# Linear attention in paired tiles: both directions, and q and k, by one instruction each

## The chip, the cores and the metric

The kernel runs on one core of a Trainium2 chip. The metric is the device time of one execution in microseconds, as the median of several runs. Five engines of the core work here side by side, each in its own order: TensorE (PE; its weight loads are shown as PEld), VectorE (DVE), ScalarE (ACT), GpSimd (POOL), and SyncE (SP), whose queue issues all of the kernel's loads. An engine goes on to its next instruction only when the one before it could start, so an instruction that waits holds up everything behind it.

## What is computed

The program is a two-layer block over 512 latent tokens behind 256 context tokens (768 in all, 1024 features). Layer 0 mixes tokens by gated linear attention in both directions, layer 1 by neighbourhood attention; a gated MLP with a short convolution follows each. Only layer 0's mixer is changed. Cut to what matters:

```python
def gla_mixer(h_ctx, h_lat, w_in, a_w1, a_w2, a_b, norm_g, w_out, with_ctx_out):
    proj = h @ w_in                                   # h: 768 tokens x 1024
    q, k, v, r = jnp.split(proj, ...)                 # 4 heads: q, k of 128, v, r of 256
    q, k = rope_2d(q[:, L:]) * dk ** -0.5, rope_2d(k[:, L:])
    for d in range(2):                                # both directions
        g = jax.nn.log_sigmoid((h @ a_w1[d]) @ a_w2[d] + a_b[d]) / 16.0
        # S_t = diag(exp(g_t)) S_{t-1} + k_t^T v_t,  o_t = q_t S_t
        o_d, _ = gla_chunked(q, k, v, g, s0)          # d == 1: on the flipped sequence
        o_sum = o_d if o_sum is None else o_sum + o_d
    y = (rms_norm(o, norm_g) * jax.nn.silu(r)).reshape(B, -1, GLA_DV) @ w_out
```

`norm_g` has one weight for each of a head's 256 value features, the same for all heads.

## The kernel before, in words

The kernel is written as tiles (named buffers from pools) and operations on them. The framework gives each engine its order when the program is built: it goes by the order in which the text emits operations, by its own estimates of durations, and by when a buffer is free, and may put an operation that is ready ahead of one emitted earlier. Loads can thus stand in SP's queue long before the text comes to them, as far as staging buffers are free. A tile with `bufs=n` has n buffers; a new one waits for the last reader of the one whose place it takes.

**Projections.** All large products are made of three products of float32r parts (`mm3`, lines 205 to 207: low by high, high by low, high by high). Weights come through `wunit` (190 to 202): a load into a staging tile `st` (line 193, three buffers), a rounded copy on ACT (`wh`, line 200), and the rest on DVE (`wl`, line 201); five pairs of `wh` and `wl` exist.

**Linear attention**, a loop over four heads (683 to 696), has two parts for each head h:

- `part_a(h)`, the levels. A chunk has 128 tokens, and the product of queries and keys inside it is built from seven levels of block size 64, 32, ..., 1. `gates_b` has left the running sums of the log gates of both directions, `b0` and `b1` (128 features x 768 tokens). A level (479 to 511) subtracts from them the value at each block's border, for queries (`eq`) and keys (`ek`), in four operations of 128x384 on DVE (491 to 494); takes the exponential of each on ACT (495, 496); multiplies by q and by k on DVE (497, 498); and multiplies the blocks on PE (`blocks_of`, 463 to 471), whose results go to `att` (504) or `attd` (507). Between levels stand one token tile's value and r projection (`vr_group`, 24 products of 128x512), one quarter of an adaLN vector (`ada_step`, 152 to 174: two loads of `sa`, line 159, two buffers, and sixteen products, line 161), and `silu_r` (557 to 567), which ends with two multiplications on POOL: r by the norm weight `gnB` (566), and by the exponential (567). Head 3 also begins the output projection there (`turn_early`, with transposes at line 591).
- `part_b(h)`, the states: decayed keys (`key_decay`, 513 to 523, for each direction) and queries (`query_decay`, 550 to 555), their transposes (`key_turn`), six chunks' states (`state`, line 542 on PE, 547 on DVE) and outputs (`output`, 578 on PE, then a norm and 584 on DVE). Between these steps stand the next head's q and k projections (`qk_group`, 422 to 434), its rotary (`rope`, 436 to 444: four small DMAs swap halves, lines 440 and 441), its gates (`gates_z`: products at line 399, `e` on ACT at 400, the minimum `mn` on DVE at 401; `gates_b`: exponential 408, logarithm 410, subtraction 411, running sums 415), and its weights. The seam between two heads is what lies around the end of `part_b` and the first level of the next head.

**Buffers that set this order.** One tag, `t3`, of six buffers of 128x768 serves `e`, `mn`, `eq`, `ek`, the decayed keys (two) and queries (two), the turned keys (two) and rope's swap. Five PSUM banks (`ps_aux`) serve the levels, gates, states, outputs, transposes and adaLN sums; three (`ps_mm`) serve the projections. q, k, b0 and b1 have one buffer each.

After the loop the output projection takes `w_go` in two halves of four tiles (675 in head 3's levels, 710 behind the loop), in which a tile of 128 x 1024 holds two groups of 128 features by 512 columns.

Of the kernel before, what the change touches and what calls it, by code (L numbers as in the profile page):

```python
# [9 lines left out]
F32 = mybir.dt.float32  # L10
# [7 lines left out]
N_LAT = 512  # L18
# [14 lines left out]
# row ranges of the packed small vectors  # L33
R_C, R_CC, R_AB, R_N1, R_N2, R_GB, R_CB, R_CW = 0, 8, 16, 112, 128, 144, 152, 196
R_END = 328
# [3 lines left out]
def body(ctx, tc, x, ctx_x, small, ada0, ada, w_gla, a_w1, a_w2, gn, w_go, w_fi, w_fo,  # L39
# [19 lines left out]
    # ---------------------------------------------------------------- constants  # L59
# [37 lines left out]
    # ---------------------------------------------------------------- adaLN vectors  # L97
# [11 lines left out]
    def ada_use(l, o, n, src):  # L109
        """Feature tiles o..o + n of layer l's adaLN vectors, from their products with the conditions."""  # L110
# [14 lines left out]
    def ada_first(q, pool):  # L125
        """256 columns (two feature tiles) of the first two adaLN vectors of layer 0; returns what is left to do."""
# [25 lines left out]
    def ada_step(l, m, i):  # L152
        """Quarter i of the contraction of adaLN vector m of layer l; returns what is left to do with it."""
# [34 lines left out]
    # ---------------------------------------------------------------- helpers  # L188
    def wunit(src, gate=None, eng=None):
        """1024 columns of weights (times a gate for each) as an exact pair of float32r tiles."""  # L190
        n = src.shape[-1]
        st = wst.tile([128, n], F32, name="st", tag="st")
        nc.sync.dma_start(st, src)
# [5 lines left out]
        lo = whl.tile([128, n], FR, name="wl", tag="wl")  # L199
        nc.scalar.activation(hi, st, AF.Copy)  # L200
# [19 lines left out]
    # the features that the projections read, as pairs of float32r: one place for all sub-layers  # L220
# [75 lines left out]
    # ================================================================ layer 0, GLA  # L296
# [44 lines left out]
    with tc.tile_pool(name="gla", bufs=6) as pool:  # L341
        def t3(dt=F32):
            return pool.tile([128, T], dt, name="t3", tag="t3", bufs=6)
# [9 lines left out]
        gnB = pool.tile([128, DV], F32, name="gnB", bufs=1)  # L353
        nc.sync.dma_start(gnB, gn.partition_broadcast(128))
# [9 lines left out]
        # w2 as rows of (high, high, low) parts against the rows (high, low, high) of the low-rank features  # L364
# [26 lines left out]
        def gates_z(h):  # L391
            st[h]["g"] = []
            for d in range(2):
                e = t3()
                mn = t3()
                bias = sT[:, R_GB + 4 * d + h:R_GB + 4 * d + h + 1]
                for a, b in RNG:
                    ps = ps_aux()
                    mm(ps[:, 0:b - a], aw2[:, d, h * 128:(h + 1) * 128], low[d][:, a:b], start=True, stop=True)
                    nc.scalar.activation(e[:, a:b], ps[:, 0:b - a], AF.Abs, bias=bias)  # L400
                    nc.vector.tensor_scalar(mn[:, a:b], ps[:, 0:b - a], bias, 0.0, OP.add, OP.min)
                st[h]["g"].append((e, mn))

        def gates_b(h):
            g = st[h].pop("g")
            st[h]["b"] = []
            for e, mn in g:
                nc.scalar.activation(e, e, AF.Exp, scale=-1.0)
            for d, (e, mn) in enumerate(g):
                nc.scalar.activation(e, e, AF.Ln, bias=1.0)  # L410
                nc.vector.tensor_sub(mn, mn, e)
# [756 lines left out]
```

## Time and profile before

| what | us |
|---|---|
| median of 3 runs | 1770.52 |
| lowest, highest | 1769.62, 1773.61 |
| span of the profiled execution | 1771.4 |
| PE busy in it | 1719.7 |
| DVE busy | 1037.1 |
| ACT busy | 663.7 |
| POOL busy | 319.7 |

The profile is of one execution; its span is 0.9 us above the median of the runs. A matmul's end is modelled in it, so a busy PE is not PE at its peak; a start, and a wait of PE, is what happened. In a group's row the name before the arrow is the tile that is written, those behind it are read; x is the count, then follow the busy time, the mean of one, and the idle time of the engine before them with what ended it. The linear attention's loop lies between about 63 and 420 us of the span.

### The profile page before, as it was taken

To read this page: it belongs to the slowest core of one execution; us is meant where nothing else is said; L and a number is where in the kernel's file an instruction comes from. 1 tells how busy PE (TensorE), PEld (TensorE's weight loads), DVE (VectorE), ACT (ScalarE), POOL (GpSimd) and SP (SyncE) were. 2 spreads that over 40 slices of the span, in tenths; PEclk is the share of its full clock that TensorE was granted. 3 is DMA by queue.
4 is the path that set the end of the run, shared out by engine and by line. 5 is a ranking of instruction groups with operands and counts; after the bars stand their busy time and mean duration, and the time that the engine had idled before them with its cause. 6 is when DMAs were issued, how large, how long until landed. Compare 5 with 4: busy or idle time off the path is not lost.

```text
span 1771.4 us, 27345 instructions
## 1 busy us (share of the span) xinstructions
PE 1719.7 (97%) x11099; PEld 1451.4 (82%) x11099; DVE 1037.1 (59%) x1599; ACT 663.7 (37%) x1225; POOL 319.7 (18%) x474
## 2 busy tenths in 40 slices
PE   6999999999999999999999999999999999999998
PEld 4767676777798999989899978888888788888887
DVE  4697767774646455564655484445445565556555
ACT  4575646552441211212122254443434432233222
POOL 2042323221100000000000023433443202222221
PEclk9999999999999999999999999999999999999999
DMA  8553525331121211212212122133232232333331
GB/s 288 154 192 120 191 84 191 93 111 72 49 95 60 72 60 48 79 59 66 63 57 72 60 66 70 50 100 103 98 107 73 84 106 80 101 107 106 92 100 48
DMA packets 50446, 169.36 MB, mean 96 GB/s; under 512 B 6608, under 2 KB 8528, under 8 KB 50320
## 3 DMA queue, kind: packets, MB, share of 16 engines
q1 hardware_dynamic: 50320, 167.62, 29.3%
q8 instruction: 87, 1.43, 0.3%
q14 instruction: 39, 0.32, 0.1%
HBM read 163.40 MB, written 2.10 MB: 93 GB/s over the span
## 4 chain that ended last, share of the span: by engine, by line
PE 80%; DVE 9%; ACT 3%; issue 2%; DMA 2%; POOL 2%; SPq 0%; DVEq 0%; POOLq 0%; ACTq 0%
PE mm L205 18%; PE mm L206 17%; PE mm L207 17%; PE aux L205 6%; PE aux L207 6%; PE aux L206 6%; PE mm L962 2%; PE aux L945 2%; PE aux L920 2%; DVE t L498 1%; PE aux L161 1%; DVE t L497 1%; PE aux L578 1%; DVE t L492 1%; PE aux L542 1%
## 5 line engine op out<-in xcount | busy, mean ns | idle before, releaser
L205 PE MATMUL mm<-hh,wl 128*128 128x384 f32 (+3 forms) x976 | 344.0, 353 | 3.8 <-ACT hh L217 2.8
L206 PE MATMUL mm<-hl,wh 128*128 128x384 f32 (+3 forms) x976 | 340.6, 349 | 0.4 <-DVE hl L218 0.4
L207 PE MATMUL mm<-hh,wh 128*128 128x384 f32 (+3 forms) x976 | 340.6, 349 | 0.0
L200 ACT ACTIVATE wh<-st 128x1024 fp32r<-128x1024 f32 (+1 forms) x197 | 204.0, 1052 | 317.7 <-issue 179.5
L201 DVE TENSOR_TENSOR wl<-st,wh 128x1024 fp32r<-128x1024 f32 (+1 forms) x196 | 242.7, 1244 | 65.0 <-ACT wh L200 43.0
L205 PEld LDWEIGHTS mm<-hh,wl 128*128 128x128 f32 (+1 forms) x976 | 183.5, 188 | 23.6 <-ACT hh L217 3.5
L206 PEld LDWEIGHTS mm<-hl,wh 128*128 128x128 f32 (+1 forms) x976 | 183.9, 188 | 20.5 <-issue 4.2
L205 PE MATMUL aux<-hh,wl 128*128 128x384 f32 (+2 forms) x576 | 200.5, 348 | 0.0
L207 PE MATMUL aux<-hh,wh 128*128 128x384 f32 (+2 forms) x576 | 200.2, 348 | 0.0
L206 PE MATMUL aux<-hl,wh 128*128 128x384 f32 (+2 forms) x576 | 200.2, 348 | 0.0
L207 PEld LDWEIGHTS mm<-hh,wh 128*128 128x128 f32 (+1 forms) x976 | 184.0, 189 | 15.0
L205 PE MATMUL mm<-wh,ul 128*128 128x512 f32 (+1 forms) x444 | 175.1, 395 | 0.0
L206 PE MATMUL mm<-wl,uh 128*128 128x512 f32 (+1 forms) x444 | 173.7, 391 | 0.0
L207 PE MATMUL mm<-wh,uh 128*128 128x512 f32 (+1 forms) x444 | 172.8, 391 | 0.0
L197 POOL TENSOR_TENSOR st<-st,gB 128x512 f32<-128x512 f32 x60 | 92.6, 1572 | 269.2 <-DMA st<-in 177.5
L788 DVE TENSOR_SCALAR tt<-apad,sT 128x769 f32<-128x769 f32 (+1 forms) x44 | 32.3, 734 | 166.7 <-ACT apad L759 166.7
L245 POOL TENSOR_SCALAR ms<-ss 128x1 f32<-128x1 f32 x26 | 8.8, 340 | 621.0 <-ACT xn L243 620.3
L205 PE MATMUL mm<-wh,hl 128*128 128x512 f32 x288 | 117.7, 409 | 2.3 <-ACT wh L200 1.7
L206 PE MATMUL mm<-wl,hh 128*128 128x512 f32 x288 | 116.0, 403 | 0.0
L205 PEld LDWEIGHTS aux<-hh,wl 128*128 128x128 f32 x576 | 108.3, 188 | 8.9 <-issue 1.8
L207 PE MATMUL mm<-wh,hh 128*128 128x512 f32 x288 | 115.7, 402 | 0.0
L206 PEld LDWEIGHTS aux<-hl,wh 128*128 128x128 f32 x576 | 108.5, 188 | 7.5 <-issue 0.4
(200 smaller groups left out, 2779.4 us busy)
## 6 DMA issues: line engine op xcount, KB each, us to landing
st<-in SPq DMA_DIRECT2D x196, 512.0 KB, 3.6
sa<-in SPq DMA_DIRECT2D x82, 512.0 KB, 4.2
sx<-in SPq DMA_DIRECT2D x14, 512.0 KB, 5.7
xl<-in SPq DMA_DIRECT2D x8, 512.0 KB, 7.7
xc<-in SPq DMA_DIRECT2D x4, 512.0 KB, 4.7
out<-xn SPq DMA_DIRECT2D x8, 256.0 KB, 2.0
raw<-in SPq DMA_DIRECT2D x16, 96.0 KB, 2.4
t<-q SPq DMA_DIRECT2D x16, 64.0 KB, 3.6
```

Of the source, the lines that this page charges most:

```text
L161: mm(ps[32 * j:32 * j + 32, 0:256], cs[:, k, :], st[:, 256 * j:256 * j + 256], start=k == 0, stop=k == KD - 1, skip_group_check=True)
L197: nc.gpsimd.tensor_mul(st[:, s_], st[:, s_], gate[half])
L200: nc.scalar.activation(hi, st, AF.Copy)
L201: (eng or nc.vector).tensor_sub(lo, st, hi.bitcast(F32))
L205: mm(out, a[1], b[0], start=first, stop=False)
L206: mm(out, a[0], b[1], start=False, stop=False)
L207: mm(out, a[0], b[0], start=False, stop=last)
L492: nc.vector.tensor_sub(v(eq)[:, :, 0, :], v(bB)[:, :, 0, :], cB)
L788: nc.vector.tensor_scalar(tt, ap_[:, 1:1 + m], cw[1], cb, OP.mult, OP.add)
L920: mm(pss[hh][:, off:off + 256], qe[a_][p_, 128 * t:128 * t + 128], ke[b_][p_, ks], start=i == 0, stop=i == 2)
L945: nc.tensor.transpose(pT[:, i * 128:(i + 1) * 128], S2[:, o:o + 128], ident)
L962: mm(po[64 * hh:64 * hh + 64, 128 * t:128 * t + 128], V[:, vs[i], 64 * hh:64 * hh + 64], PTs[hh][:, i * 128:(i + 1) * 128], start=i == 0, ...
```

## The change

Three things, all in layer 0's mixer:

- *Pairs.* Tiles of 128 x 768 become tiles of 128 x 2 x 768 (`t6`, three buffers in place of `t3`'s six): e and mn for both directions; the gates' running sums in one tile `bb`, backward first; q and k in one tile `qk`; a level's `eq` and `ek`; decayed keys, turned keys and decayed queries for both directions. One instruction then does for both what two did: the exponential, logarithm and subtraction of the gates, the exponential and the multiplication of a level, of the keys' decay and of the queries' decay. A level's four subtractions become two of 128x768, through an access pattern written by hand that steps between the two halves of `bb`; for keys the order of the subtraction is turned round, so that one scale serves both exponentials. Rope's swap gets a tile of its own with one buffer.
- *Norm weights.* `gnB`, its load and the POOL multiplication by it go. The norm weight comes as two columns with the packed small vectors and multiplies the rows of `w_go` as these are converted: in two halves on ACT (with a scale) and on DVE (scalar_tensor_tensor).
- *Loads.* The loads of the next head's q and k weights are emitted behind the first products of `part_a`, ahead of the levels; their conversion stays behind the levels.

Comments are removed too. The core of the diff:

```diff
+    def wload(src):
+        st = wst.tile([128, src.shape[-1]], F32, name="st", tag="st")
+        nc.sync.dma_start(st, src)
+        return st
...
+        if scales:
+            for half in range(2):
+                s_ = slice(half * 512, half * 512 + 512)
+                nc.scalar.activation(hi[:, s_], st[:, s_], AF.Copy, scale=scales[half])
+                nc.vector.scalar_tensor_tensor(lo[:, s_], st[:, s_], scales[half], hi[:, s_].bitcast(F32), OP.mult,
+                                               OP.subtract)
+            return hi, lo
...
-        def t3(dt=F32):
-            return pool.tile([128, T], dt, name="t3", tag="t3", bufs=6)
+        def t6():
+            return pool.tile([128, 2, T], F32, name="t6", tag="t6", bufs=3)
...
         def gates_z(h):
+            e, mn = t6(), t6()
             for d in range(2):
...
-                    nc.scalar.activation(e[:, a:b], ps[:, 0:b - a], AF.Abs, bias=bias)
-                    nc.vector.tensor_scalar(mn[:, a:b], ps[:, 0:b - a], bias, 0.0, OP.add, OP.min)
+                    nc.scalar.activation(e[:, d, a:b], ps[:, 0:b - a], AF.Abs, bias=bias)
+                    nc.vector.tensor_scalar(mn[:, d, a:b], ps[:, 0:b - a], bias, 0.0, OP.add, OP.min)
...
+            e, mn = st[h].pop("g")
+            nc.scalar.activation(e, e, AF.Exp, scale=-1.0)
+            nc.scalar.activation(e, e, AF.Ln, bias=1.0)
+            nc.vector.tensor_sub(mn, mn, e)
+            bb = pool.tile([128, 2, T], F32, name="bb", tag="bb", bufs=1)
...
+                    nc.vector.tensor_tensor_scan(bb[:, 1 - d, a:b][:, ::step], reset, mn[:, d, a:b][:, ::step], 0.0,
                                                  OP.mult, OP.add)
...
+        def qk_load(h):
+            st[h]["raw"] = [wload(w_gla[h, i]) for i in range(2)]
...
-            sw = t3()
+            sw = pool.tile([128, N_LAT], F32, name="sw", tag="sw", bufs=1)
...
         def level(h, li):
...
-            nc.vector.tensor_sub(v(eq)[:, :, 1, :], v(bF)[:, :, 1, :], cF)
-            nc.vector.tensor_sub(v(eq)[:, :, 0, :], v(bB)[:, :, 0, :], cB)
-            nc.vector.tensor_sub(v(ek)[:, :, 0, :], v(bF)[:, :, 0, :], cF)
-            nc.vector.tensor_sub(v(ek)[:, :, 1, :], v(bB)[:, :, 1, :], cB)
-            nc.scalar.activation(eq, eq, AF.Exp, scale=1.0 / GATE)
-            nc.scalar.activation(ek, ek, AF.Exp, scale=-1.0 / GATE)
-            nc.vector.tensor_mul(eq, eq, st[h]["q"])
-            nc.vector.tensor_mul(ek, ek, st[h]["k"])
+            def at(first, second, inner=1):
+                return bass.AP(bb.tensor, base + first, [lead, [2 * s, n], [second - first, 2], [inner, s]])
+            e = t6()
+            eq, ek = (e[:, i, :].rearrange("p (n two s) -> p n two s", two=2, s=s) for i in range(2))
+            nc.vector.tensor_sub(eq, at(0, T + s), at(s, T + s - 1, 0))
+            nc.vector.tensor_sub(ek, at(T + s - 1, s, 0), at(T, s))
+            nc.scalar.activation(e, e, AF.Exp, scale=1.0 / GATE)
+            nc.vector.tensor_mul(e, e, st[h]["qk"])
...
         def key_decay(h):
+            kd = t6()
+            for d in range(2):
+                nc.vector.tensor_sub(ch(kd[:, d, :]), ch(bb[:, 1 - d, :]),
+                                     last[:, d, :, :].to_broadcast([128, NCH, CH]))
             nc.scalar.activation(kd, kd, AF.Exp, scale=-1.0 / GATE)
+            nc.vector.tensor_mul(kd, kd, st[h]["qk"][:, 1:2, :].to_broadcast([128, 2, T]))
...
         def silu_r(h, c):
...
-            nc.gpsimd.tensor_mul(yh, yh, gnB)
             nc.gpsimd.tensor_mul(yh, yh, e)
...
             diag(h)
+            if h < HEADS - 1:
+                qk_load(h + 1)
             for i in range(7):
                 level(h, i)
...
-                wo[0] = [wunit(w_go[0, q]) for q in range(4)]
+                wo[0] = [wunit(w_go[0, q], scales=gn_cols) for q in range(4)]
```

More of the change, by code (lines that the diff above doesn't have):

```diff
@@ L34, with body @@
 R_C, R_CC, R_AB, R_N1, R_N2, R_GB, R_CB, R_CW = 0, 8, 16, 112, 128, 144, 152, 196
-R_END = 328
+R_GN = 328
+R_END = 330
 @with_exitstack
-def body(ctx, tc, x, ctx_x, small, ada0, ada, w_gla, a_w1, a_w2, gn, w_go, w_fi, w_fo,
+def body(ctx, tc, x, ctx_x, small, ada0, ada, w_gla, a_w1, a_w2, w_go, w_fi, w_fo,
          w_nqk, w_no, rpb, fg, ident_d, rope_d, lvl_d, nmask_d, *outs):
@@ L186, in gate_rows, with wunit @@
         return out
-    def wunit(src, gate=None, eng=None):
+    def wload(src):
+        st = wst.tile([128, src.shape[-1]], F32, name="st", tag="st")
+        nc.sync.dma_start(st, src)
+        return st
+    def wunit(src, gate=None, eng=None, scales=None):
         n = src.shape[-1]
-        st = wst.tile([128, n], F32, name="st", tag="st")
-        nc.sync.dma_start(st, src)
+        st = wload(src) if src.space == bass.MemoryType.DRAM else src
         if gate:
@@ L352, in body @@
         nc.vector.tensor_copy(lvl, lst)
-        gnB = pool.tile([128, DV], F32, name="gnB", bufs=1)
-        nc.sync.dma_start(gnB, gn.partition_broadcast(128))
+        gn_cols = [sT[:, R_GN + i:R_GN + i + 1] for i in range(2)]
         two_i = pool.tile([128, 32], F32, name="two_i", bufs=1)
@@ L525, in key_turn, with key_decay @@
-        def key_turn(h, d):
-            kd = st[h].pop(("kd", d))
-            kt = t3()
-            for c0, c1 in ((0, 4), (4, 6)):
+        def key_decay(h):
+            bb = st[h]["b"]
+            last = bass.AP(bb.tensor, bb.offset + T + CH - 1, [bb.ap[0], [1 - CH - T, 2], [CH, NCH], [0, 1]])
+            ed = sml.tile([128, 2, NCH], F32, name="ed", tag="ed", bufs=2)
+            nc.scalar.activation(ed, last.rearrange("p d c o -> p d (c o)"), AF.Exp, scale=1.0 / GATE)
+            kd = t6()
+            for d in range(2):
+                nc.vector.tensor_sub(ch(kd[:, d, :]), ch(bb[:, 1 - d, :]),
+                                     last[:, d, :, :].to_broadcast([128, NCH, CH]))
+            nc.scalar.activation(kd, kd, AF.Exp, scale=-1.0 / GATE)
+            nc.vector.tensor_mul(kd, kd, st[h]["qk"][:, 1:2, :].to_broadcast([128, 2, T]))
+            st[h]["kd"] = kd
+            st[h]["ed"] = ed
@@ L529, in key_turn @@
+        def key_turn(h):
+            kd = st[h].pop("kd").rearrange("p d t -> p (d t)")
+            kt = t6()
+            st[h]["kt"] = kt
+            kt = kt.rearrange("p d t -> p (d t)")
+            for c0 in range(0, 2 * NCH, 4):
                 ps = ps_aux()
-                for c in range(c0, c1):
+                for c in range(c0, c0 + 4):
                     nc.tensor.transpose(ps[:, (c - c0) * CH:(c - c0 + 1) * CH], kd[:, c * CH:(c + 1) * CH], ident)
-                nc.scalar.activation(kt[:, c0 * CH:c1 * CH], ps[:, 0:(c1 - c0) * CH], AF.Copy)
@@ L533, in key_turn @@
-            st[h]["kt", d] = kt
-            st[h]["S", d] = {}
+                nc.scalar.activation(kt[:, c0 * CH:c0 * CH + 512], ps, AF.Copy)
+            for d in range(2):
+                st[h]["S", d] = {}
         ORDER = ((0, 1, 2, 3, 4, 5), (1, 0, 5, 4, 3, 2))
@@ L541, in state @@
             ps = ps_aux()
-            mm(ps[:, 0:DV], st[h]["kt", d][:, c * CH:(c + 1) * CH], st[h]["v", c], start=True, stop=True)
+            mm(ps[:, 0:DV], st[h]["kt"][:, d, c * CH:(c + 1) * CH], st[h]["v", c], start=True, stop=True)
             s_new = pool.tile([128, DV], F32, name=f"S{d}", tag=f"S{d}", bufs=5 if d else 3)
@@ L546, in state @@
             else:
-                nc.vector.scalar_tensor_tensor(s_new, S[c], st[h]["ed", d][:, c, :], ps[:, 0:DV], OP.mult, OP.add)
+                nc.vector.scalar_tensor_tensor(s_new, S[c], st[h]["ed"][:, d, c:c + 1], ps[:, 0:DV], OP.mult, OP.add)
             S[order[i + 1]] = s_new
         def query_decay(h):
-            for d in range(2):
-                e = t3()
-                nc.scalar.activation(e, st[h]["b"][d], AF.Exp, scale=1.0 / GATE)
-                nc.vector.tensor_mul(e, e, st[h]["q"])
-                st[h]["qd", d] = e
+            e = t6()
+            nc.scalar.activation(e, st[h]["b"], AF.Exp, scale=1.0 / GATE)
+            nc.vector.tensor_mul(e, e, st[h]["qk"][:, 0:1, :].to_broadcast([128, 2, T]))
+            st[h]["qd"] = e
         def silu_r(h, c):
@@ L709, in finish_gla @@
             add_gated(pool, ps, (g_ctx if t < 2 else g_lat)[0], X[t][:, 0:512])
-        wo[1] = [wunit(w_go[1, q]) for q in range(4)]
+        wo[1] = [wunit(w_go[1, q], scales=gn_cols) for q in range(4)]
         for t in range(6):
```

71 lines of the change are left out of this document (21 added, 50 removed).

## The prediction

> **What bounds the kernel now.** I read the page first, then busy time by stretch, the waits of TensorE (PE), the chain of work that ended last, and the order of time on VectorE (DVE) and on the DMA queue of SyncE (SP). The page's first lines:
>
> ```profile
> span 1771.4 us, 27345 instructions
> PE 1719.7 (97%) x11099; PEld 1451.4 (82%) x11099; DVE 1037.1 (59%) x1599; ACT 663.7 (37%) x1225; POOL 319.7 (18%) x474
> L200 ACT ACTIVATE wh<-st 128x1024 fp32r<-128x1024 f32 (+1 forms) x197 | 204.0, 1052 | 317.7 <-issue 179.5
> ```
>
> PE is busy 97% of the span, so an edit off PE can only win back PE's waits. 1771.4 - 1719.7 = 51.7 us is the most there is, and the change touches only the linear attention. By stretch (start:end, length, then busy PE, PEld, DVE, ACT, POOL, and PE's granted clock), head 0's levels, head 1's levels, head 1's states, head 3's levels:
>
> ```profile
> 90.00:124.00 34.00, 30.97 (x487) 19.22 (x486) 33.36 (x51) 23.73 (x47) 11.66 (x11) 1.00 0.57 184
> 165.00:207.00 42.00, 39.86 (x535) 28.97 (x535) 41.69 (x63) 29.75 (x59) 12.21 (x10) 1.00 0.44 138
> 207.00:252.00 45.00, 41.28 (x262) 34.27 (x261) 21.69 (x35) 17.76 (x40) 9.77 (x16) 0.92 0.43 141
> 338.00:380.00 42.00, 39.59 (x555) 28.78 (x551) 41.32 (x64) 29.48 (x60) 13.60 (x13) 1.00 0.32 101
> ```
>
> In the levels DVE is busy 41.69 of 42.00 us and PE 39.86: both are nearly full, DVE a little fuller. In the states DVE has half its time free and PE waits 45.00 - 41.28 = 3.7 us. PE's waits over the whole linear attention (total, times, longest), the chain at the seam of head 1, and SP's issues there:
>
> ```profile
> PE aux L161 <- DMA sa<-in: 8.4, 7, 3.7
> PE aux L469 <- DVE t L498: 6.3, 7, 1.4
> PE aux L591 <- DVE attd L507: 2.3, 1, 2.3
> ```
>
> ```profile
> 205.10 1.14 DVE wl L201
> 206.69 5.06 DMA sa<-in
> 211.79 1.08 PE aux L161 x8
> ```
>
> ```profile
> 151.66 0.38 SPq L193 DMA_DIRECT2D st<-in  x1
> 204.26 2.33 SPq L193 DMA_DIRECT2D st<-in  x2
> 206.69 1.31 SPq L159 DMA_DIRECT2D sa<-in  x2
> ```
>
> One late engine makes two waits. PE waits 6.3 us for level products (L469) because DVE is full. It waits 8.4 us for adaLN weights (sa) because SP, in order, holds their issue behind weight loads (st), and those wait for a staging buffer that DVE's conversion (L201) frees. So the bound is DVE in the levels, and what shortens DVE there counts until PE itself is full.
>
> **Fewer, larger instructions.** DVE back to back without disturbance, and the two exponentials of a level on ScalarE (ACT):
>
> ```profile
> 256.83 0.56 DVE L491 TENSOR_TENSOR t<-b 128x384 f32<-128x384 f32 x1
> 257.29 0.96 DVE L497 TENSOR_TENSOR t<-t,q 128x768 f32<-128x768 f32 x1
> 258.16 0.95 DVE L498 TENSOR_TENSOR t<-t,k 128x768 f32<-128x768 f32 x1
> ```
>
> ```profile
> 256.01 0.85 ACT L495 ACTIVATE t<-t 128x768 f32<-128x768 f32 x1 [1.14 <-DVE t L492]
> ```
>
> From start to start a 384-wide operation takes 257.29 - 256.83 = 0.46 (0.47 with the unrounded rest) and a 768-wide one 258.16 - 257.29 = 0.87 us. Each 384 more cost 0.40, and 0.07 is fixed, so a 1536-wide one takes 1.67. A level has four subtractions and two multiplications, 4 x 0.47 + 2 x 0.87 = 3.62; afterwards two and one, 2 x 0.87 + 1.67 = 3.41. Seven levels save 7 x 0.21 = 1.5. The decays' four multiplications become two: 3.48 - 3.34 = 0.1. Together 1.6 us of DVE per head.
>
> [...] The starts decide: the durations overlap, and 0.07 is what an instruction costs.
>
> **The norm weight's multiplication leaves POOL.** While POOL multiplies, DVE's operations take longer. DVE and POOL in head 1's levels (us busy, mean ns):
>
> ```profile
> L497 DVE TENSOR_TENSOR t<-t,q 128x768 f32<-128x768 f32 x7 | 7.2, 1027 | 0.0
> L498 DVE TENSOR_TENSOR t<-t,k 128x768 f32<-128x768 f32 x7 | 7.1, 1010 | 0.0
> ...
> L494 DVE TENSOR_TENSOR t<-b 128x384 f32<-128x384 f32 x7 | 4.9, 706 | 0.0
> L492 DVE TENSOR_TENSOR t<-b 128x384 f32<-128x384 f32 x7 | 4.9, 706 | 0.0
> L493 DVE TENSOR_TENSOR t<-b 128x384 f32<-128x384 f32 x7 | 4.4, 628 | 0.0
> L491 DVE TENSOR_TENSOR t<-b 128x384 f32<-128x384 f32 x7 | 4.4, 627 | 0.0
> L521 DVE TENSOR_TENSOR t<-t,k 128x768 f32<-128x768 f32 x2 | 2.4, 1224 | 0.0
> ```
>
> ```profile
> L566 POOL TENSOR_TENSOR xl<-xl,gnB 128x256 f32<-128x256 f32 x3 | 3.4, 1123 | 15.6 <-DVE er L564 15.6
> L567 POOL TENSOR_TENSOR xl<-xl,er 128x256 f32<-128x256 f32 x3 | 3.2, 1066 | 0.2
> ```
>
> Against the undisturbed 0.555 and 0.955 us these are too long by 7 x (0.072 + 0.055 + 0.151 + 0.151 + 0.073 + 0.072) + 2 x 0.269 = 4.6 us per head. A head's r takes twelve POOL multiplications, six of them by gnB (L566). Without these six DVE gets back between 0 and 4.6; I take half, 2.3, since L566 and L567 are alike in size and duration. DVE's relief is 1.6 + 2.3 = 3.9 us per head, 15.6 for four.
>
> **The gates between heads get later.** The seam after head 1, on DVE and on PE:
>
> ```profile
> 244.57 1.14 DVE L401 TENSOR_SCALAR t<-aux,sT 128x384 f32<-128x384 f32 x2
> ...
> 246.80 1.15 DVE L401 TENSOR_SCALAR t<-aux,sT 128x384 f32<-128x384 f32 x2
> 247.86 0.48 DVE L584 SCALAR_TENSOR_TENSOR xl<-aux,rs,xl 128x256 f32<-128x256 f32 x1
> 248.25 0.86 DVE L547 SCALAR_TENSOR_TENSOR S<-S,ed,aux 128x256 f32<-128x256 f32 x2
> 249.03 1.80 DVE L415 TENSOR_TENSOR_SCAN b<-reset,t 128x384 f32<-128x384 bf16 x2
> 250.75 0.94 DVE L411 TENSOR_TENSOR t<-t,t 128x768 f32<-128x768 f32 x1
> ```
>
> ```profile
> 245.43 0.59 PE L542 MATMUL aux<-V,t 128*128 128x256 f32 x2
> ...
> 246.09 0.59 PE L542 MATMUL aux<-V,t 128*128 128x256 f32 x2
> ...
> 246.75 0.39 PE L207 MATMUL mm<-wh,hh 128*128 128x512 f32 x1
> 246.98 0.40 PE L205 MATMUL mm<-wh,hl 128*128 128x512 f32 x1
> ```
>
> Six single buffers become three double ones. At the seam they hold the decayed queries, the turned keys and e; mn needs the turned keys' buffer, free after the last state (L542, 246.09 + 0.59 = 246.7). Today one direction's minimum has run by then (244.57), and the other waits (246.80). Afterwards both wait. After the release DVE has two minima more (247.86 - 246.80 = 1.06) and a doubled L411 (0.80), but L584 and one L547 (0.39 + 0.39) fall before it: 1.1 later. Also, the four gate products hold four of five aux banks until their minima; today the two at 244.57 free the banks in which the states at 245.43 and 246.09 run. Afterwards the states share the bank of the output before them, free after its L584, now at about 246.8 + 0.5 = 247.3. Two states in turn, each 0.59 on PE with a 0.5 evacuation between, end at 249.0, not 246.7: 2.3 later. The bank's share lies between 0 (another order) and 2.3; the nearest rows are these, so I take 2.3. That is 3.4 us per seam, 10.2 for three. Queued behind it on DVE are the scans and all of the next levels; PE has value products meanwhile.
>
> **The rest.** In head 0 the doubled L411 stands ahead of the scans: +0.8. The scaled output weights cost ACT a second start: from 0.85 at 768 columns and 1.052 at 1024 (0.79 ns a column) a start is 0.24, four times 1.0 us for the first half's weights, where PE already waits 2.3 (L591); between 0 and 1.0, I take 0.5. The second half's conversions stand beside a full PE: 0, otherwise 1.0. Rope's single swap buffer makes k's swap follow q's: hidden in head 0 by four subtractions of level 0 (1.9, the cost without that cover). The early q and k loads, moved ahead of the levels' 14 adaLN loads on SP, I cost at 0: the staging buffers are already filled that early, the last at 151.66, with the next issue at 204.26 only when conversions free one. Fewer key-turn copies, one decay factor instruction and the gnB load gone: off the path, 0.
>
> **Sum**: -15.6 + 10.2 + 0.8 + 0.5 = -4.1 us on the chain through DVE. PE can follow: head 0 (-3.9 + 0.8) has 34.00 - 30.97 = 3.0 us of waits, the others need 3.9 - 3.4 = 0.5 each. The profiled span is 0.9 us above the median of the runs, 1770.5 (1769.6 to 1773.6); the difference is applied to that: 1766.4.
>
> **Rivals.** (1) *The adaLN wait falls too*: if the build's order lets DVE's conversion gain on PE by the 3.9 us of a head, the 8.4 us of sa waits go, and so does the half clock that follows:
>
> ```profile
> 211.30:218.00 6.70, 6.21 (x30) 4.06 (x31) 0.10 (x1) 0.56 (x2) 2.11 (x4) 0.50 0.75 243
> ```
>
> 6.7 us at 0.50 lose 3.4. Then -4.1 - 8.4 - 3.4 = -15.9: 1754.6. For it: the chain. Against it: after head 0 a head's net gain is 0.5 us, not 3.9. [...]
>
> (2) *Nothing is won*: larger pieces expose latency. A level's first product waits for a 1.45 us exponential (0.85 + 768 x 0.79 ns) and a 1.67 us multiplication where pieces overlapped; 0.6 + 0.8 later at each of four heads is 5.6, which eats the 4.1 and 1.5 more: 1772. For it: PE's waits for L498. Against it: DVE has other levels to do, three in flight as now.
>
> (3) *Slower, by the banks*: a state that wants the one free bank is placed on PE behind a group of 24 value products (one each 246.98 - 246.75 = 0.23 us, so 5.5). The seam is then 8.9 later; in two seams of three that is 11.0 more, and -4.1 becomes +6.9: 1777. It turns the sign from 4.1 / 3 = 1.4 us per seam beyond my 3.4. Against it: PE's rows show states put between single value products.
>
> **How the numbers follow.** A measurement here can tell about 0.2%, 3.5 us. The forecast has 0.45 (1762 to 1770.5, of which 0.28 beyond 3.5 us faster), rival 1 0.17, rival 2 0.18, rival 3 0.20. Faster 0.28 + 0.17 = 0.45; within 0.2% 0.17 + 0.16 = 0.33; slower 0.20 + 0.02 = 0.22. The range of 8 in 10 runs from 1752 (rival 1 and 2 us) to 1777 (the price of rival 3).
>
> **What would show it.** Right: L566 gone and the level subtractions' means near 0.96 us; DVE's busy time in the levels down by some 4 us; minima (L401) in one run of four after the last state. Wrong: levels as full as before, PE waiting for states' banks, or sa waits gone altogether.

## The result, and the profile after

The changed kernel takes 1774.68 us (median of 18 runs, 1771.42 to 1777.69) against 1771.22 us (18 runs beside them, 1765.49 to 1774.06): a ratio of 1.0019, 95% interval [1.0011, 1.0027]. It is slower by 0.19%, 3.4 us. The forecast was 4.1 us faster. The medians of the kernel before, on the chips used here, lie between 1770.8 and 1771.8, so kernels are compared below by their ratios to the runs of the kernel before on the same chip; 0.1% is 1.8 us.

The profiled execution after, its span and the share of each engine:

```profile
span 1773.1 us, 27174 instructions
...
PE 1718.0 (97%) x11099; PEld 1447.0 (82%) x11099; DVE 1022.4 (58%) x1511; ACT 658.1 (37%) x1181; POOL 324.8 (18%) x450
```

DVE has lost 88 instructions and 14.7 us of busy time over the whole program. The forecast's 15.6 is another sum (start to start, in the four heads), but of the same size, and the kernel is still no faster. POOL has 24 instructions fewer and is busy 5.1 us longer. The stretches that answer to those shown of before (start:end, length, then busy PE, PEld, DVE, ACT, POOL, and the granted clock), from the first to the last block product of a head: head 0's levels, head 1's levels, its states up to the next head's first block product, head 3's levels:

```profile
76.40:124.50 48.10, 42.95 (x572) 30.83 (x571) 42.03 (x47) 32.59 (x58) 11.85 (x5) 0.96 0.45 139
165.80:209.20 43.40, 40.27 (x577) 28.32 (x576) 40.52 (x45) 28.79 (x53) 16.77 (x9) 1.00 0.42 131
209.20:254.70 45.50, 42.37 (x229) 35.18 (x225) 19.65 (x32) 17.54 (x36) 7.69 (x13) 0.96 0.43 143
342.60:387.30 44.70, 41.10 (x551) 28.57 (x550) 39.71 (x48) 28.18 (x55) 16.08 (x9) 0.96 0.35 107
```

Head 1's levels before, cut in the same way:

```profile
162.80:205.10 42.30, 40.16 (x580) 28.97 (x579) 41.55 (x65) 29.51 (x61) 13.73 (x13) 1.00 0.40 126
```

They have grown from 42.3 us to 43.4 although DVE in them does less, and POOL, with half of its multiplications gone, is busy 16.77 us in them. PE's waits, then POOL's last multiplication of silu_r (mean ns after the comma, first two token tiles and the others), then ACT's waits for it:

```profile
PE aux L162 <- DMA sa<-in: 14.1, 14, 2.5
PE aux L481 <- DVE t L507: 6.0, 4, 1.9
PE aux L557 <- DVE xl L597: 1.8, 3, 0.6
```

```profile
L580 POOL TENSOR_TENSOR xc<-xc,er 128x256 f32<-128x256 f32 x8 | 40.4, 5067 | 61.6 <-ACT er L579 61.6
L580 POOL TENSOR_TENSOR xl<-xl,er 128x256 f32<-128x256 f32 x16 | 19.0, 1188 | 54.4 <-ACT er L579 54.1
```

```profile
ACT er L575 <- POOL xc L580: 15.7, 5, 6.7
```

The last two in the kernel before:

```profile
L567 POOL TENSOR_TENSOR xl<-xl,er 128x256 f32<-128x256 f32 x16 | 17.2, 1074 | 1.3
L567 POOL TENSOR_TENSOR xc<-xc,er 128x256 f32<-128x256 f32 x8 | 9.7, 1207 | 5.7 <-ACT er L565 5.3
```

```profile
ACT er L561 <- POOL xc L567: 2.1, 2, 1.7
```

Three things stand out. The wait for adaLN weights (sa) did not fall; it rose from 8.4 to 14.1 us. The wait for level products is as it was, 6.3 and now 6.0. And POOL's multiplication lasts 5.07 us on average on the first two tiles (1.21 before), so that ACT, in order, stands still for its result for 15.7 us, where it was 2.1 before.

The seam after head 1, on DVE and on PE, shows what the prediction had foreseen:

```profile
249.36 0.48 DVE L597 SCALAR_TENSOR_TENSOR xl<-aux,rs,xl 128x256 f32<-128x256 f32 x1 [3.26 <-POOL rs L226]
250.64 0.48 DVE L562 SCALAR_TENSOR_TENSOR S<-S,ed,aux 128x256 f32<-128x256 f32 x1 [0.79 <-PE aux L557]
251.91 2.19 DVE L412 TENSOR_SCALAR t<-aux,sT 128x384 f32<-128x384 f32 x4 [0.79 <-PE aux L557]
...
261.41 0.95 DVE L504 TENSOR_TENSOR t<-bb 128x768 f32<-128x768 f32 x1
```

```profile
249.90 0.70 PE L557 MATMUL aux<-V,t 128*128 128x256 f32 x2 [0.61 <-DVE xl L597]
...
251.18 0.70 PE L557 MATMUL aux<-V,t 128*128 128x256 f32 x2
...
254.73 0.26 PE L481 MATMUL aux<-qk 128*32 128x32 f32 x6
```

All four minima (L412) run in one go, right behind the last state (251.18 + 0.70), and DVE idles ahead of them. States wait for the bank that an output holds (0.61). From the first turned key to the end of the last state it is now 251.9 - 219.0 = 32.9 us (29.9 before). The next head's first level subtraction (L504) starts 261.41 - 254.73 = 6.7 us behind its first block product. In head 1 that distance was 3.7 us before (L491 at 166.45, first block product at 162.8).

### The profile page after: what moved, and what is told of

The parts are those of the page before. It is cut to its first block, busy times and chain, and to the rows that moved or that the text cites. A ratio compares the mean times of both kernels' runs of the same rounds, so it can differ in the third digit from the quotient of the medians.

```text
span 1773.1 us, 27174 instructions
## 1 busy us (share of the span) xinstructions
PE 1718.0 (97%) x11099; PEld 1447.0 (82%) x11099; DVE 1022.4 (58%) x1511; ACT 658.1 (37%) x1181; POOL 324.8 (18%) x450
## 4 chain that ended last, share of the span: by engine, by line
PE 85%; DMA 4%; DVE 3%; POOL 2%; issue 2%; ACT 2%; DVEq 0%; SPq 0%; POOLq 0%; ACTq 0%
PE mm L218 18%; PE mm L220 18%; PE mm L219 18%; PE aux L218 6%; PE aux L219 6%; PE aux L220 6%; DMA sa<-in 4%; PE aux L162 2%; PE mm L975 2%; PE aux L933 2%; PE aux L958 1%; PE aux L591 1%; PE aux L557 1%; DVE bb L425 1%; PE aux L284 1%
## 5 line engine op out<-in xcount | busy, mean ns | idle before, releaser
L213 ACT ACTIVATE wh<-st 128x1024 fp32r<-128x1024 f32 (+1 forms) x189 | 196.0, 1052 | 302.6 <-issue 179.5
L214 DVE TENSOR_TENSOR wl<-st,wh 128x1024 fp32r<-128x1024 f32 (+1 forms) x188 | 234.6, 1253 | 62.2 <-ACT wh L213 40.7
L801 DVE TENSOR_SCALAR tt<-apad,sT 128x769 f32<-128x769 f32 (+1 forms) x44 | 31.9, 725 | 165.8 <-ACT apad L772 165.8
```

Source lines behind the costliest of these rows:

```text
L214: (eng or nc.vector).tensor_sub(lo, st, hi.bitcast(F32))
L801: nc.vector.tensor_scalar(tt, ap_[:, 1:1 + m], cw[1], cb, OP.mult, OP.add)
```

## The experiments

Each was timed in five rounds beside the kernel before. Theory A is POOL's starved multiplication with ACT behind it, theory B the seam between heads, theory C the two buffers of the adaLN weights.

**POOL out of the levels (e1, e2).** The first moves one multiplication, the second the whole of silu_r.

```diff
-            nc.gpsimd.tensor_mul(yh, yh, e)
+            nc.vector.tensor_mul(yh, yh, e)
```

> The changed kernel with silu_r's one multiplication (yh by e) on DVE instead of POOL: no POOL work in the levels. Theory A (POOL's multiplication is starved by DVE's back-to-back merged instructions, and ACT, in order, waits for the er buffer that it holds): ACT's wait for POOL (15.7 us over the kernel) is gone, at the price of 6 x 0.48 = 2.9 us of DVE per head less the 2.1 of contention that was left, so some 0.8 us more DVE per head; the kernel is 2 to 6 us faster than the changed one, about 1769 to 1773. Theory B (the seam between heads carries the loss: the gates' minima wait for the turned keys' buffer, states share a bank): the seams stay and DVE only gets more to do, 1775 to 1780. Theory C (the two adaLN buffers bind by themselves): PE's waits for sa stay near 14 us and the time near 1775.

Measured: 1768.8 us, ratio 0.9984 [0.9972, 0.9996], 6 us faster than the changed kernel. ACT's waits for POOL are gone; PE's sa waits stay at 13.7.

```diff
 # part_a
-                if i > 0:
-                    silu_r(h, i - 1)
 # part_b: silu_r(h, 0), (h, 1) after other(0); (h, 3) after other(1); (h, 4) after other(2); (h, 2), (h, 5) after other(3)
```

> The changed kernel with all of silu_r moved from the levels to the states, ahead of the outputs that use it, where DVE has half its time free. Theory A: the levels lose the POOL contention (2.1 us per head), ACT's waits for POOL, and 6 x 0.4 = 2.4 us of DVE per head, so they become PE-bound at some 41 us instead of 43.4 to 48; time 1758 to 1768. Theory B: the seam, already the cost, gets 6 x 4 ACT activations of about 0.45 us (10.8 us) more per head in ACT's order ahead of key turns and state copies: 1776 to 1785. Theory C: sa waits stay at 14 us, the levels shorten little, 1772 to 1776.

Measured: 1766.9 us, 0.9963 [0.9948, 0.9978], 10 us faster by the ratio, within A's range. So taking POOL's multiplication out of the levels is worth 6 us in the changed kernel, and taking all of silu_r out, with ACT's and DVE's part of it, 10 us. It is not the whole loss, as the next runs show.

**The parts by themselves (e3, e4).** e3 takes the kernel before and drops gnB's multiplication, with the output weights scaled as in the change. e4 is the change without that part; a multiplication of the same size by the cosine table stands in for the one by gnB, and the norm weights are left out of its result.

```diff
 # e3, in the kernel before
-            nc.gpsimd.tensor_mul(yh, yh, gnB)
...
-                wo[0] = [wunit(w_go[0, q]) for q in range(4)]
+                wo[0] = [wunit(w_go[0, q], scales=gn_cols) for q in range(4)]
 # e4, in the changed kernel
+            nc.gpsimd.tensor_mul(yh, yh, cosT[:, 0:DV])
             nc.gpsimd.tensor_mul(yh, yh, e)
```

> The kernel before with the norm weight's part alone: gnB's multiplication gone from silu_r, output weights scaled, tiles and loads as before. Theory A: DVE's instructions stay small and leave gaps, so POOL's remaining multiplications still take about 1.1 us, ACT does not wait, and DVE gets back about half of its 4.6 us of contention per head: 1762 to 1768. Theory B: it has nothing to do with the seam, so the gain of 1762 to 1768 would come too, and the loss must then show in the next kernel. Rival D (scaling the output weights costs what it saves): 1770 to 1773.

> The changed kernel with a second multiplication of the same size back on POOL in silu_r (by the first 256 columns of the cosine table in place of the norm weights) and the output weights unscaled, so paired tiles and early loads without the norm weight's part; the norm weights are not applied. Theory A: two starved multiplications per chunk, ACT waits longer for POOL than the 15.7 us of the changed kernel; 1778 to 1786. Theory B: the seams are the loss and unchanged, DVE's contention as before the change: 1775 to 1779. Theory C: like the changed kernel, 1773 to 1776.

Measured: e3 1759.7 us, 0.9925 [0.9907, 0.9942]; e4 1781.2 us, 1.0045 [1.0032, 1.0059]. The norm weights' part alone gains 0.75%, 13 us, and the tiles in pairs cost 8 us without it and 0.94%, 17 us, on top of it. So the change is a gain and a larger loss, and the loss lies in the pairs. Head 0's and head 1's levels in e3 (columns as above), and POOL's multiplication in it:

```profile
76.00:121.00 45.00, 42.00 (x581) 28.27 (x580) 41.96 (x68) 32.38 (x67) 6.79 (x6) 1.00 0.49 156
159.40:201.30 41.90, 40.05 (x580) 28.95 (x579) 40.42 (x66) 30.56 (x63) 7.75 (x8) 1.00 0.43 137
```

```profile
L573 POOL TENSOR_TENSOR xc<-xc,er 128x256 f32<-128x256 f32 x8 | 9.4, 1178 | 76.9 <-ACT er L572 76.9
```

Beside DVE's small instructions POOL needs 1.18 us, not 5.07.

**The levels' instructions unmerged (e5).** Pair tiles, loads and scaled weights stay.

```diff
-            nc.vector.tensor_sub(eq, at(0, T + s), at(s, T + s - 1, 0))
-            nc.vector.tensor_sub(ek, at(T + s - 1, s, 0), at(T, s))
-            nc.scalar.activation(e, e, AF.Exp, scale=1.0 / GATE)
-            nc.vector.tensor_mul(e, e, st[h]["qk"])
+            def one(off, inner=1):
+                return bass.AP(bb.tensor, base + off, [lead, [2 * s, n], [inner, s]])
+            nc.vector.tensor_sub(eq[:, :, 1, :], one(T + s), one(T + s - 1, 0))
+            nc.vector.tensor_sub(eq[:, :, 0, :], one(0), one(s, 0))
+            nc.vector.tensor_sub(ek[:, :, 0, :], one(T + s - 1, 0), one(T))
+            nc.vector.tensor_sub(ek[:, :, 1, :], one(s, 0), one(s))
+            for i in range(2):
+                nc.scalar.activation(e[:, i, :], e[:, i, :], AF.Exp, scale=1.0 / GATE)
+            for i in range(2):
+                nc.vector.tensor_mul(e[:, i, :], e[:, i, :], st[h]["qk"][:, i, :])
```

> The changed kernel with the paired tiles, early loads and scaled output weights kept, but a level's instructions as before: four subtractions of 384, two exponentials and two multiplications of 768, each on its half of the paired tile. Theory A (the long two-input instructions without gaps starve POOL): POOL's multiplication, 5.07 us mean on the first two chunks now, returns to 1.2 to 1.5, ACT's 15.7 us of waits for it fall to 2, DVE has 1.5 us per head more to do; 3 to 9 us faster than the changed kernel, 1766 to 1772. Theory B (the seam: shared buffers and banks) and theory C (two adaLN buffers, early loads): POOL may be served sooner, but the time stays, 1774 to 1778.

Measured: 1773.7 us, 1.0012 [0.9998, 1.0027], no different from the changed kernel. POOL and ACT in it:

```profile
L587 POOL TENSOR_TENSOR xl<-xl,er 128x256 f32<-128x256 f32 x16 | 31.3, 1957 | 57.9 <-ACT er L586 57.7
L587 POOL TENSOR_TENSOR xc<-xc,er 128x256 f32<-128x256 f32 x8 | 11.8, 1470 | 82.8 <-ACT er L586 82.8
```

```profile
ACT er L582 <- POOL xc L587: 3.7, 2, 3.3
```

On the first tiles POOL's delay goes with the long instructions: with short ones its multiplication is back to 1.47 us there (5.07), and ACT's wait falls from 15.7 to 3.7, while on the other tiles it takes 1.96 (1.19). The time does not follow, against what A expected: whatever merging saved on DVE and whatever it cost through POOL come out even here.

**The gates in one buffer (e6, and e11 and e15 as controls).** -ln(1 + exp(-z)) needs no second tile; the signs of the later exponentials turn. e6 has no guard against overflow, which the minimum is in the original; in e11 (the kernel before) and e15 (e3) z is kept above -80 by the same instruction.

```diff
-            e, mn = t6(), t6()
+            e = t6()
...
-                    nc.scalar.activation(e[:, d, a:b], ps[:, 0:b - a], AF.Abs, bias=bias)
-                    nc.vector.tensor_scalar(mn[:, d, a:b], ps[:, 0:b - a], bias, 0.0, OP.add, OP.min)
+                    nc.vector.tensor_scalar(e[:, d, a:b], ps[:, 0:b - a], bias, None, OP.add)
...
-            nc.vector.tensor_sub(mn, mn, e)
```

> The changed kernel with the gates' logarithm of the sigmoid as -ln(1 + exp(-z)), without the guard of the minimum against overflow: one paired tile instead of two, no minimum's buffer that waits for the turned keys, 1.7 us less DVE per seam. Theory A: the seam gives back 1 to 3 us of its 3.65, POOL is starved as in the changed kernel: 1768 to 1773, less than half of the way to the 1759.7 of the norm weights alone. Theory B: the seam falls back to that of the kernel before and the time with it: 1762 to 1767. Theory C: 1773 to 1775.

> The kernel before with the gates as -ln(1 + exp(-z)), z kept above -80 by the same instruction, so one tile per direction and no minimum and no subtraction: the control to the same edit of the changed kernel, which gained 20 us. Theory B1 (the buffer's wait in the paired tiles): no such wait here, only some 3 us of DVE less per head beside free DVE time: 1766 to 1770. Theory B2 (fewer instructions at the seam): 1752 to 1760.

> The kernel before with the norm weights' part and the gates in one tile per direction (z kept above -80), so the run with the gates in one buffer (1754.6 us) without paired tiles. If pairing is worth its 6 us once the seam's wait is gone: 1758 to 1762. If pairing gains nothing: 1752 to 1756. If it still costs: 1746 to 1751.

Measured: e6 1754.6 us, 0.9901 [0.9884, 0.9917], faster than any theory had it; e11 1761.4 us, 0.9939 [0.9920, 0.9957], between B1 and B2; e15 1755.0 us, 0.9901 [0.9878, 0.9924]. The edit gains 21 us in the changed kernel and 11 in the one before, but in e3, which differs from the changed kernel by the pairs (and the early loads) alone, it gains only 0.24%, 4 us (each of these to within 3 to 5 us). So shorter gates are worth some 4 us there, and the other 17 hang on the second paired tile that the gates no longer need: as much as the pairs cost on top of e3. With the gates in one buffer, pairs (e6) and no pairs (e15) take the same time. The 6 us by which pairs ought to have won are not there either.

**The wait by itself (e9).** The cleanest run: no instruction fewer, only another tile for the minima, one that is free since the query decay.

```diff
-            e, mn = t6(), t6()
+            e = t6()
+            mn = pool.tile([128, 2, T], F32, name="bb", tag="bb", bufs=1)
...
-            bb = pool.tile([128, 2, T], F32, name="bb", tag="bb", bufs=1)
+            bb = mn
```

> The changed kernel with the gates' minima written into the tile in which the scans end (free since the query decay, scanned in place) instead of a third paired buffer: same instructions, no wait for the turned keys' buffer. Theory B1 (the minima's wait for that buffer, with the banks that the gate products hold meanwhile, is the loss of the seams): key turn to last state falls from 31 to 33 us back to 29 or less and the time to 1756 to 1766. Theory B2 (the gain of the run with one buffer came from its 1.7 us less of DVE and four activations fewer per seam): 1771 to 1775. Theory A (POOL): 1771 to 1775 too.

Measured: 1760.3 us, 0.9935 [0.9918, 0.9953], 0.84% or 15 us faster than the changed kernel, of the 17 that the pairs cost. The seam after head 1 on DVE, then head 1's levels and its states:

```profile
236.32 2.19 DVE L413 TENSOR_SCALAR bb<-aux,sT 128x384 f32<-128x384 f32 x4
...
250.62 0.95 DVE L505 TENSOR_TENSOR t<-bb 128x768 f32<-128x768 f32 x1
```

```profile
164.20:205.60 41.40, 39.67 (x580) 29.09 (x579) 36.48 (x42) 29.76 (x52) 5.79 (x5) 1.00 0.43 141
205.60:249.50 43.90, 41.36 (x224) 34.53 (x223) 22.95 (x35) 16.66 (x36) 9.74 (x17) 0.96 0.44 145
```

The minima run at 236.32, 5.3 us ahead of the last state's end (241.6). The first level subtraction follows the first block product by 250.62 - 249.50 = 1.1 us, not 6.7. That is less than the 3.7 of the kernel before: e9 takes away more than the pairs had added, since in the kernel before one direction's minimum waited too. In the levels DVE is busy 36.48 of 41.40 us: it has room again. In head 1 POOL is quick too:

```profile
173.43 0.94 POOL L581 TENSOR_TENSOR xc<-xc,er 128x256 f32<-128x256 f32 x1 [11.52 <-ACT er L580]
182.39 0.94 POOL L581 TENSOR_TENSOR xc<-xc,er 128x256 f32<-128x256 f32 x1 [8.03 <-ACT er L580]
```

In the levels of heads 1 and 3 POOL is busy 5.79 and 6.09 us, where it was 16.77 and 16.08 in the changed kernel. So there the starving goes with the wait. That POOL starves because DVE is late is not shown, though: in e6, whose gates are early, POOL's mean on the first tiles is still 3.6 us, and only ACT's waits for it are gone (1.3 us):

```profile
L578 POOL TENSOR_TENSOR xc<-xc,er 128x256 f32<-128x256 f32 x8 | 28.8, 3606 | 62.1 <-ACT er L577 62.1
```

The sa waits in e9 fall to 7.6.

**On top of it (e13, e14).** e13 is e9 with e1's edit, e14 is e9 with e5's.

> The run with the minima in the scans' tile (1760.3 us), and silu_r's multiplication on DVE besides. If POOL's hold on ACT in head 0 (one wait of 6.6 us there) still costs: 2 to 5 us faster than that run, 1755 to 1758. If DVE's 2.9 us more per head weigh as much: 1759 to 1762.

> The run with the minima in the scans' tile, and the levels' instructions unmerged as in the kernel before. If merging shortens the levels as the prediction reckoned (1.5 us of DVE per head): some 6 us slower, 1765 to 1767. If merging gains nothing, because what it saves on DVE comes back as POOL's and ACT's waits and larger pieces: 1758 to 1762.

Measured: e13 1757.0 us, 0.9915 [0.9897, 0.9934]; e14 1761.0 us, 0.9941 [0.9924, 0.9957]. Both intervals overlap with e9's. Head 0, in which POOL still holds ACT for 6.6 us in e9, may be worth the 3.5 us of e13. Merging is worth 0.06%, 1 us, by the middle values; the two intervals together leave room for some 5. Head 1's levels show why it can't be much: unmerged they take 41.2 us in e14 with DVE busy 38.4, merged 41.4 in e9 with DVE busy 36.5, and PE is busy 39.6 and 39.7 in them. It is PE that is full there.

**The adaLN loads (e7, e10, e8, e16).** In e7 (the changed kernel) and e10 (the one before) both products of a step read one tile, so half of the loads are left out.

```diff
         for k in (2 * i, 2 * i + 1):
-            st = ast.tile([128, 1024], F32, name="sa", tag="sa")
-            nc.sync.dma_start(st, ada[6 * l + m - 2, k])
+            if k % 2 == 0:
+                st = ast.tile([128, 1024], F32, name="sa", tag="sa")
+                nc.sync.dma_start(st, ada[6 * l + m - 2, k])
```

> The changed kernel with every second load of adaLN weights left out (both products of a step read the first tile; the adaLN vectors are then not the reference's). Theory A: waits for sa partly follow ACT's and DVE's delay, so that of PE's 14.1 us of sa waits some 10 go but POOL's hold on ACT stays: 1764 to 1769. Theory C (two buffers bind by themselves): all 14 us go and the time is 1758 to 1763. Theory B: 1770 to 1774, since other waits take their place.

> The kernel before with every second load of adaLN weights left out (the adaLN vectors are not the reference's), as the control to the same edit of the changed kernel, which gained 17.7 us. Theory C1 (the two adaLN buffers bind only since the levels start later and ask for them closer together): it gains its 8.4 us of sa waits at most, 1761 to 1768. Theory C2 (they bind in both alike, so they carry none of the loss): it gains as much, 1752 to 1757.

Measured: e7 1756.9 us, 0.9914 [0.9896, 0.9932], a little below C's range; e10 1759.2 us, 0.9928 [0.9912, 0.9943]. The loads bind in both kernels, 19 us in the changed one and 13 in the one before, between C1 and C2. With half of them gone the two kernels are alike, although e7 still has the late seams (6.7 us) and ACT's waits for POOL (13.5 us). Whether these cost nothing where PE need not also wait for sa, or are made up by the norm weights' gain, which e7 has and e10 has not, is not shown: no run halves the loads of e3.

```diff
-            if h < HEADS - 1:
-                qk_load(h + 1)
...
-            st[h]["w", i] = wunit(st[h]["raw"][i])
+            st[h]["w", i] = wunit(w_gla[h, i])
```

> The changed kernel with the loads of the next q and k weights back where the weights are converted, after the levels. Theories A and B: the loads wait for staging buffers either way, no change from the changed kernel within 2 us, 1773 to 1777. Rival E (the early loads sit on SP ahead of the levels' adaLN loads and hold them): PE's sa waits fall from 14.1 towards 8.4 us and the time to 1766 to 1770.

Measured: 1772.9 us, 1.0007 [0.9993, 1.0021], within what can be told from the changed kernel: the early loads cost little or nothing.

e16 gives e6 (z kept above -80) four buffers of half the size:

```diff
-    ast = ctx.enter_context(tc.tile_pool(name="ast", bufs=2))
+    ast = ctx.enter_context(tc.tile_pool(name="ast", bufs=4))
...
+            for p in range(2):
-            st = ast.tile([128, 1024], F32, name="sa", tag="sa")
-            nc.sync.dma_start(st, ada[6 * l + m - 2, k])
+                st = ast.tile([128, 512], F32, name="sa", tag="sa")
+                nc.sync.dma_start(st, ada[6 * l + m - 2, k][:, 512 * p:512 * p + 512])
```

> The run with the gates in one buffer (z kept above -80), and the adaLN weights in four buffers of half the size, the same bytes in twice as many loads. If the two buffers' turnaround (3.5 to 5.5 us from issue to landing for each) sets the 10.3 us of sa waits: 1746 to 1751. If the number of loads on SP or the bytes set it: 1754 to 1759.

Measured: 1766.4 us, 0.9966 [0.9952, 0.9979], 12 us slower than e6 and beyond both expectations. The sa waits did fall, from 10.3 to 6.3 us, and all of PE's waits in the program from 38.4 to 34.0, but the profiled span rose from 1752.8 to 1765.2: PE spends 16.8 us more outside of waits. The reason stays open.

**Combinations (e12, e17, e18).** e12 is e6 (z kept above -80) with e2's edit.

> The changed kernel with the gates in one buffer (z kept above -80) and all of silu_r in the states: both of the gains so far, a version meant to beat both kernels. If POOL's hold (7.8 us gained alone) and the seam (20 us alone) are separate losses: 1745 to 1750. If they are two ways to the same slack of PE: 1752 to 1756.

Measured: 1757.2 us, 0.9914 [0.9895, 0.9933], no better than e6, and above both expectations: with the gates in time, moving silu_r gives nothing more. e17 and e18 move two adaLN steps of a head from the levels to the states, in the changed kernel and in e6 (z kept above -80).

```diff
-                todo = ada_step(*blocks.pop(0)) if h < HEADS - 1 or i < 4 else None
+                todo = ada_step(*blocks.pop(0)) if i < (5 if h < HEADS - 1 else 4) else None
 # part_b, after other(1) and before other(4)
+            if h < HEADS - 1:
+                ada_step(*blocks.pop(0))()
```

> The changed kernel with two of the seven adaLN steps of a head's levels moved to its states, so five stand in the levels and three in the states; the same loads in all. If the late gates cost time because the levels' adaLN loads are squeezed (half the loads gave 17.7 us): the sa waits of 14.1 us fall below 6 and the time to 1760 to 1767. If the seam's wait costs by itself, wherever the loads stand: 1771 to 1775. If the loads meet the weight loads in the states: 1775 to 1780.

> The run with the gates in one buffer (z kept above -80), and two of seven adaLN steps of a head moved to its states. A version meant to beat both kernels: if its 10.3 us of sa waits go, 1745 to 1750; if PE is full without them or the loads meet the weight loads, 1753 to 1758.

Measured: e17 1785.9 us, 1.0076 [1.0062, 1.0090]; e18 1746.4 us, 0.9856 [0.9843, 0.9869], the fastest, 1.4% below the kernel before. One edit, once 10 us slower (beyond all three expectations) and once 8 faster. In e17 the sa waits fall as hoped, and PE waits for DVE instead:

```profile
PE aux L481 <- DVE t L507: 17.4, 7, 4.0
PE aux L162 <- DMA sa<-in: 5.0, 8, 1.4
```

The way there, in head 1 of e17, one row each from POOL, ACT (two), DVE and PE, in order of time (in brackets the idle time ahead of it), and the stretch behind it:

```profile
182.34 5.54 POOL L580 TENSOR_TENSOR xc<-xc,er 128x256 f32<-128x256 f32 x1 [9.75 <-ACT er L579]
```

```profile
187.91 0.42 ACT L575 ACTIVATE er<-xl 128x256 f32<-128x256 f32 x1 [4.44 <-POOL xc L580]
...
190.59 1.48 ACT L506 ACTIVATE t<-t 128x1536 f32<-128x1536 f32 x1
```

```profile
192.10 3.96 DVE L507 TENSOR_TENSOR t<-t,qk 128x1536 f32<-128x1536 f32 x2 [4.81 <-ACT t L506]
```

```profile
193.92 0.87 PE L481 MATMUL aux<-t 128*32 128x32 f32 x48 [3.84 <-DVE t L507]
```

```profile
193.00:199.80 6.80, 5.88 (x117) 3.40 (x117) 6.25 (x9) 3.54 (x8) 2.38 (x2) 0.50 0.20 46
```

POOL's multiplication, 5.54 us long beside DVE's unbroken run, holds the `er` buffer; ACT waits 4.4 us for it with the level's exponential queued behind; DVE waits 4.8 us for the exponential, PE 3.8 us for DVE, and then runs 6.8 us at half clock (0.50). Theory A's mechanism is all there, in a kernel whose gates are late. In e18 they are early, ACT's waits for POOL come to 1.3 us, and head 1's levels and states show a PE that is full, 38.21 of 39.20 and 40.58 of 40.70 us:

```profile
160.00:199.20 39.20, 38.21 (x564) 28.82 (x563) 31.93 (x35) 28.68 (x51) 8.32 (x5) 1.00 0.44 147
199.20:239.90 40.70, 40.58 (x238) 34.00 (x238) 25.61 (x41) 16.29 (x34) 10.81 (x17) 1.00 0.50 158
```

## Why the prediction was wrong

The sum was -15.6 (DVE's relief: 6.4 by merging, 9.2 by the norm weights) + 10.2 (seams) + 0.8 (head 0) + 0.5 (scaled weights). By the runs it is -13 for the norm weights with their scaling (e3), about 0 for merging (e5, e14, and e15 beside e6), +15 for the seams' buffer (e9), and some 2 that are left and that the intervals (0.17% or 3 us to each side) cover: +3.4. The time lies inside the stated range, but the sign is wrong, and three terms are off by 4 to 6 us each, not all the same way.

- **The bound, half right.** The forecast had DVE in the levels as the bound "until PE itself is full". PE was full sooner than that. Head 1's levels take 41.9 us in e3, 41.4 in e9, 41.2 in e14 and 40.3 in e6, with DVE busy 40.4, 36.5, 38.4 and 34.0 of them, and PE 40.1, 39.7, 39.6 and 39.3: their length follows PE, not DVE.
- **Merging, the step that failed: "DVE's relief is 1.6 + 2.3 = 3.9 us per head, 15.6 for four".** The relief itself came. In head 1, from the first level subtraction to the end of the key decays' multiplications, DVE took 38.6 us before (166.45 to 205.03) and 37.0 after (172.50 to 209.48). Without weight conversions (1.7 and 2.8) and idle time (0.3 and 2.2), its work there fell from 36.6 to 32.0 us, by 4.6 where 3.9 was reckoned. But it was summed as time, and of the 4.6 only 1.6 are left in the elapsed time even here. The part by merging gave none, within the intervals, in any of three pairs of kernels. With late gates waits took its place (DVE's idle time above, 15.7 us of ACT's waits, 3.7 unmerged); with gates in time PE is full and DVE's relief is worth nothing.
- **The norm weights, right and too small.** 2.3 us a head, 9.2, less 0.5, was forecast, 13 measured (10 to 16 by the interval). What DVE's operations in e3's levels take beyond their undisturbed times (0.555 and 0.955 us) is 1.8 to 2.4 us a head in heads 1 to 3, where it was 3.9 to 4.6: about half, as reckoned. Where the rest of the 13 comes from is not shown.
- **The seams, seen, and priced too low.** From the key turn to the last state they grew by 2.4, 3.0 and 3.5 us, and by 1.3 more from there to the first level subtraction (in head 1's seam 251.9 to 261.41, where it was 246.7 to 254.96). That is 3.6 to 4.8 us each, 12.7 in all, for a forecast of 3.4 and 10.2. Taking the wait away gave 15 us, but e9's three seams are also 8.0 us shorter in all than those of the kernel before, so 15 is not the price of the growth alone. The forecast let DVE's lateness and its relief cancel on one chain, but the lateness also moved the first adaLN step of head 1 from 171.5 - 162.8 = 8.7 us behind the first block product to 179.0 - 165.8 = 13.2, and PE's sa waits rose from 8.4 to 14.1 us. That the loads through two buffers come closer together then is the likely link (in e9 that step is back to 171.7 - 164.2 = 7.5 us and the sa waits to 7.6), but e7 and e10 do not settle it.
- **Head 0: +0.8 was forecast on top of 3.9 gained.** From its first block product to head 1's it went from 86.7 to 89.4 us. POOL's hold of ACT, in the chain of work that ended last the longest piece of head 0's first levels, was nowhere in the forecast (start, us, what):

```profile
87.53 7.10 POOL xc L580
```

- **Early loads at 0: right** (e8, within what can be told). Scaled weights: inside e3's gain, their own cost was not measured.
- **The rivals.** That sa waits would fall, and the half clock with them: they rose, and half clock came at three places in the changed kernel's levels and states (0.50 for 3.4 us from 98.9, 215.0 and 368.6), though none of its sa waits is longer than 2.5 us, where the forecast's row stood behind one of 3.7. That larger pieces expose latency: nothing was won by merging, as this rival had it, but not by its mechanism, since PE's waits for level products are 6.0 us merged, 6.3 before, and 7.0 and 6.8 in e9 and e14. Slower by the banks: the sign is right, but the states' waits for a bank are three of 0.6 us. How much of the 15 us is the banks that the gate products hold and how much the minima's lateness stays open, since both go together in e9.

## What to carry to other kernels

A merge that shares buffers in pairs also ties their releases together: ask of each pair what its later half waits for, and look for a tile that is free by then, before counting saved instructions. An engine's saved time is worth time only where that engine is late; measure each part of a change by itself, since a gain of 13 us and a loss of 17 look like nothing much. And where an in-order engine that feeds two others (ACT here) waits through a two-buffer tag for a third engine's spare work, as it does here for POOL, its delay can travel on to both (in e17 4.4 us of ACT's waiting were followed by 4.8 of DVE's and 3.8 of PE's).

## What was not expected of the hardware

At two places POOL's short instruction lasted about as long as DVE ran two-input instructions without a gap. A 256-wide multiplication, 0.94 us in e9's rows above, took 5.54 in e17's, and 5.07 on average on the first tiles of the changed kernel. In e17 DVE's unbroken run ends at 187.29, and POOL's multiplication at 187.88; in the changed kernel's head 0 (7.09 us from 87.53) they end at 94.29 and 94.62. Both multiplications took longer than any one DVE instruction there (1.75 us for 1536 elements in e17, 0.96 in head 0). It is not always so: the next multiplication in e17, at 192.45, took 2.00 us, though DVE ran on without a gap to 197.54.

Halving an adaLN load did not halve its time: 512 KB took 4.2 us, 256 KB 3.6. DMA issues (count, KB each, median us from issue to landing) in the changed kernel and in e16:

```profile
sa<-in SPq DMA_DIRECT2D x56, 512.0 KB, 4.2
```

```profile
sa<-in SPq DMA_DIRECT2D x112, 256.0 KB, 3.6
```
